# Holding the first input transfers behind the first weight split, and moving two groups of small products, in a one-core decoder layer

## The chip, the core and the metric

The kernel runs on one core of a Trainium2 chip. The core has a matrix engine (TensorE, PE in the profile; its loads of stationary operands are PEld), a vector engine (VectorE, DVE), a scalar engine (ScalarE, ACT), a general engine (GpSimd, POOL) and an engine that here issues nearly all transfers (SyncE, SP). Each engine runs its own list of instructions in a fixed order and waits on semaphores for the others. The metric is device time in microseconds, the median of the runs shown. A change of 0.2% (2.4 us here) is about what can be told from no change.

## The reference

One layer of a decoder trunk on 1024 tokens of width 1024, float32:

```python
h = rmsnorm(x, norm1_w)
proj = h @ w_in                      # q, k, v, z, beta, gate of mixer A; q, k, v of mixer B
qkv_a = silu(causal_dwconv(qkv_a, conv_qkv_w))      # 4 taps
qa, ka = l2norm(qa) * 128**-0.5, l2norm(ka)
o_a = gated_delta_rule(qa, ka, va, g, beta)         # 4 heads of 128, chunks of 64
o_a = rmsnorm(o_a, gdn_norm_w) * silu(z)
o_b = dilated_attention(qb, kb, vb)                 # 8 heads of 64, 3 windows
x = x + concat(o_a, o_b) @ w_out
u = causal_dwconv(rmsnorm(x, norm2_w) @ w_up, ffn_conv_w)   # 3 taps
x = x + (silu(gate) * up) @ w_down
return rmsnorm(x, final_norm_w)
```

The change touches the first norm, the projection to the first three keys of mixer A, and the start of the delta rule.

## The kernel before, in words

Every large product of float32 operands is made as three products of rounded parts: each operand is split into a high part (`...hi`, a copy on ACT) and a low part (`...lo`, the difference on DVE), and PE adds high x high, high x low and low x high. Channels lie on partitions, tokens along the free axis. So a 128x128 weight block against 512 tokens costs three products of 128x512.

The stretch up to about 70 us runs as follows.

- **Loads.** The input comes as eight channel tiles `xt` (128 channels x 1024 tokens, 512 KB; the first in two halves), the weights of the first three keys as four pairs `wst` (two channel blocks x 384 columns, 384 KB; the first pair in two halves of 192 KB). Each engine that issues transfers feeds its own queue. The two halves of the first weights leave from ACT, everything else from SP.
- **Splits.** `split_first` splits weights, `split_x` splits an input tile and scales it with `norm1_w` on the way. Squares of the tiles (`sq`) are summed into `acc` on DVE for the norm.
- **First products.** Before its data is there PE runs nine products `warm`. `first()` then adds, channel tile by channel tile, six accumulators (three keys x two halves of the tokens): 18 products for each tile.
- **Norm and gates.** `norms()` sums `acc` over the channels with eight small products (`ps<-ones,acc`), POOL raises the result to -0.5 (`rst`), PE spreads it over the partitions by eight transposes (`ps<-ident,rst`), and DVE copies that out as `rstdB`. `gates()` makes decay and beta from `wba` and the unscaled tiles (`ps<-xt,wba`), then `ps<-sel,barow` and `ps<-g,tri`.
- **Keys.** DVE multiplies each accumulator by `rstdB` (`xr`). `conv_silu` then makes a key: ACT scales by the first tap (`kT<-xr,gcw`), DVE adds three taps (`kT<-xr,gcw,kT`), ACT takes a tanh (`xr<-kT`), DVE finishes (`kT<-xr,kT`). `kprep(h)` takes the finished key: `tokens()` transposes it on PE (`ps<-ident,kT`, two halves of four), ACT copies each half out and squares it (`ktok`, `sq`), DVE makes the scales (`ssk`, `bp`, `ke`), and PE multiplies the key with itself in two halves of four (`ps<-kT`), which DVE turns into `um`. On the side POOL masks the decay rows `dec` and ACT takes their exponentials. All transposes and key products of this stage share two PSUM banks of the tag `atr`.
- **Dense products.** Between these small pieces PE works through the products of the remaining weights, which begin with the fourth key and then the values.

What sets the order: `Weave` is a planner that runs while the kernel is recorded. It keeps a clock of PE and estimated ready times of tiles (`need`) and of banks (`slot_free`); each stream of work is a generator that yields the time it still has to wait, with `slack` added. The order in which streams reach PE in that plan is the order of PE's instructions (each gets an issue order token). On ACT, DVE, POOL and SP the order is set by the scheduler of the framework, with `ua` and `uv` for work of high priority and `after(a, b)` for pairs that must keep an order. `A(name, tag)` takes a slot of a tag; a slot is reused in turn, and a transfer into it waits for the last reader of its former content. The four weight pairs take turns in the two slots of the tag `wst`.

Of the kernel before, what the change touches and what calls it, by code (L numbers as in the profile page):

```python
# [7 lines left out]
F32 = mybir.dt.float32  # L8
# [7 lines left out]
P = 128  # L16
# [4 lines left out]
FT = 22  # L21
NEG = -1.0e30
APART = 0.5
KSLACK = 1.0
EPS = 1e-6
SLOTS = {"kT": 2, "kU": 2, "dv": 2, "dw": 2, "kt": 4, "uy": 5, "qa": 4, "ev": 2, "go": 2, "Xa": 7, "Xb": 9}
TURNS = {"kT*": ("kT", "kU"), "dv*": ("dv", "dw"), "X": ("Xa",) * 7 + ("Xb",) * 9}
# [120 lines left out]
def hybrid_layer(tc, I, out):  # L148
    nc = tc.nc
    wv = Weave()  # L150
# [5 lines left out]
    po_ = Engine(wv, nc.gpsimd, "gpsimd", 0.15, 0.0021)  # L156
    sy = Engine(wv, nc.sync, "sync", 0.05, 0.00142, 2.2)
    sa = Engine(wv, nc.scalar, "actq", 0.05, 0.00142, 2.2)
    es = ExitStack()
    cp = es.enter_context(tc.tile_pool(name="cp", bufs=1))  # L160
    wp = es.enter_context(tc.tile_pool(name="wp", bufs=1))
# [5 lines left out]
    def tile_(pool, shape, dt, name, tag, bufs):  # L167
        return wv.slot(pool.tile(list(shape), dt, name=name, tag=tag, bufs=bufs), tag, bufs)
# [3 lines left out]
    def A(name, tag, dt=F32, shape=(P, 1024)):  # L172
        if tag in TURNS:
            i = turns[tag] = turns.get(tag, -1) + 1
            tag = TURNS[tag][i % len(TURNS[tag])]
        return tile_(lp, shape, dt, name, tag, SLOTS[tag])

    def X(name, dt=F32R):
        return A(name, "X", dt)
# [7 lines left out]
    order = mybir.DependencyInfo(mybir.DependencyClass.NoSync, mybir.DependencyReason.DATA)  # L187

    def after(inst, anchor, reason="keeps a slot free until it is needed"):
        tc.add_manual_dep(inst.ins, anchor.ins.name, order, reason=reason)  # L190
# [83 lines left out]
    def half(i):  # L274
        return slice(i * 512, i * 512 + 512)
# [8 lines left out]
    acc = A("acc", "go")  # L284
    wk0 = []

    def split_x(xt, k, sl):
        hi, lo = xs[k]
        inst = ua.activation(hi[:, sl], xt[:, sl], AF.Copy, scale=n1[:, k:k + 1])
        if k == 0:  # L290
            after(inst, his[0] if sl.start else whis[0], "in the order of arrival")
        if k == 1:
            after(inst, whis[1], "the weights come first")
        his[k:] = [inst]
        lo_of[0] = uv.scalar_tensor_tensor(lo[:, sl], xt[:, sl], n1[:, k:k + 1], hi[:, sl].bitcast(F32), op0=OP.mult,
                                           op1=OP.subtract)

    def split_first(src, hi, lo):
        whis.append(ua.activation(hi, src, AF.Copy))
        return uv.tensor_tensor(lo, src, hi.bitcast(F32), op=OP.subtract)  # L300

    his, los, lo_of, sqs, whis = [], [], [None], [], []
# [11 lines left out]
    for k in range(KT):  # L314
        xt = A("xt", ("kT*", "dv*")[k % 2])
        xts.append(xt)
        if k % 2 == 0:
            wst = tile_(wp, [P, 2, 384], F32, "wst", "wst", 2)
            whi, wlo = [A(nm, "uy", F32R, (P, 2, 384)) if k < 4 else A(nm, "kt", F32R, (P, 2, 384))
                        for nm in ("whi", "wlo")]  # L320
            wk0.append((whi, wlo))
        xs.append((X("xhi"), X("xlo")))
        if k == 0:
            for j in range(2):
                sa.dma_start(wst[:, j, :], I["w0"][0, :, j])
            for h in range(2):
                sy.dma_start(xt[:, half(h)], I["xT"][:P, half(h)])
            split_first(wst[:, 0, :], whi[:, 0, :], wlo[:, 0, :])
            for h in range(2):
                split_x(xt, 0, half(h))  # L330
            split_first(wst[:, 1, :], whi[:, 1, :], wlo[:, 1, :])
        else:
            if k % 2 == 0:
                sy.dma_start(wst, I["w0"][k // 2])
            sy.dma_start(xt, I["xT"][k * P:(k + 1) * P, :])
            if k % 2 == 0:
                split_first(wst, whi, wlo)
            split_x(xt, k, slice(0, S))
        los.append(lo_of[0])
        if k > 1:  # L340
            square(k - 2, his[k], los[k])
# [55 lines left out]
    rstdB = const("rstdB", [P, S])  # L397

    def norms():
        yield wv.need(acc, slack=9.5)  # L400
        ssp = yield from next_bank("atr", acc)
        for c in range(NCH):
            mm(ssp[:, c:c + 1], acc[:, c * P:(c + 1) * P], ones[:, :1], 0.215)
            if c % 2:
                yield APART
        ve.tensor_scalar(rst, ssp[:, :NCH], 1.0 / 1024, EPS, op0=OP.mult, op1=OP.add)
        rsqrt(rst, rst, NCH)
        wv.done.add("rst")
        yield wv.need(rst)
        for h in range(2):  # L410
            if h:
                yield wv.need(rstdB, slack=0.3)
            pb = yield from next_bank("atr")
            for c in range(4):
                i = 4 * h + c
                tp(pb[:, c * P:(c + 1) * P], rst[:, i:i + 1].to_broadcast([P, P]))
            ve.tensor_copy(rstdB[:, half(h)], pb)
        wv.done.add("norms")
# [211 lines left out]
    def kprep(h):  # L630
# [44 lines left out]
        for c0 in range(0, NCH, 4):  # L675
            pt = yield from next_bank("atr", slack=KSLACK * (c0 == h == 0))
            for c in range(4):
# [1007 lines left out]
```

## Time and profile before

| | |
|---|---|
| median of 3 runs | 1202.02 us (1200.88 to 1202.2) |
| profiled execution, its own time | 1201.61 us |
| span of that execution, first to last instruction | 1199.6 us |
| granted clock of PE over the span | 0.998 |
| PE busy | 1186.8 us, 99% |
| DVE, ACT, POOL busy | 915.6, 574.8, 87.2 us |
| DMA moved | 154.80 MB, 129 GB/s on average |
| DMA from 8 to 12 us | 417 GB/s |

All times of the trace count from the start of the span. In a row of the timeline stand start, length, engine, line, operation, output and inputs, shapes, count, and in brackets the idle time of the engine just before it with what ended that idle time. The operations recorded through the `Engine` helper all carry line 142 or 144, and those of PE line 193 or 197, so they are told apart by their tiles. Products overlap: a product of 128x512 shows 0.39 us, while the next starts 0.227 us after it.

### The profile page before, as it was taken

The page shows a single profiled execution, that of the slowest core. Times are in us where ns is not written, and L with a number is a line of the kernel's source. Part 1 is how long each engine was busy: PE and PEld are TensorE (multiplying, and loading weights), DVE is VectorE, ACT ScalarE, POOL GpSimd, SP SyncE. Part 2 cuts the span into 40 slices and gives each one's busy share as a digit, 9 for nine tenths or more (in the row PEclk, how much of TensorE's full clock was granted, in tenths as well). Part 3 has the DMA queues.
Part 4 walks back from the last instruction along what each step waited for, and adds up shares of the span by engine and source line. Part 5 has one row for each costly group of instructions (what it writes and reads, how often), then busy time and mean ns, then how long its engine had stood idle before and what let it go on. Part 6 is the DMA issues. An engine that isn't in the chain of part 4 may idle for free.

```text
span 1199.6 us, 18291 instructions
## 1 busy us (share of the span) xinstructions
PE 1186.8 (99%) x7050; PEld 983.1 (82%) x7050; DVE 915.6 (76%) x1450; ACT 574.8 (48%) x1126; POOL 87.2 (7%) x90
## 2 busy tenths in 40 slices
PE   9999999999999999999999999999999999999997
PEld 7788888888777778888888888888888888888886
DVE  7683975666365566777989988989888889999875
ACT  7375344355454443655544544445454454434441
POOL 0212010214311120000000000000000000000000
PEclk9999999999999999999999999999999999999999
DMA  7424334435634204443213223131222398557514
GB/s 234 110 87 122 109 118 129 141 123 171 224 100 124 80 28 129 163 158 122 88 53 105 83 76 105 54 105 56 103 87 72 101 375 295 187 159 225 166 54 140
DMA packets 85799, 154.80 MB, mean 129 GB/s; under 512 B 21169, under 2 KB 36305, under 8 KB 85713
## 3 DMA queue, kind: packets, MB, share of 16 engines
q1 hardware_dynamic: 84704, 152.72, 39.4%
q8 instruction: 55, 0.90, 0.3%
q10 hardware_dynamic: 1008, 0.92, 0.2%
q14 instruction: 32, 0.25, 0.1%
HBM read 117.68 MB, written 35.93 MB: 128 GB/s over the span
## 4 chain that ended last, share of the span: by engine, by line
PE 93%; DVE 2%; DMA 1%; ACT 1%; issue 1%; SPq 0%; POOLq 0%; POOL 0%; DVEq 0%; ACTq 0%
PE ps L193 44%; PE pa L193 20%; PE dw L193 17%; PE pc L193 10%; PE ps L197 3%; DVE kT L142 1%; DMA xt<-in_xT 1%; ACT sm L144 0%; DVE xr L142 0%; DMA alog<-in_a_log 0%; DMA n<-in_n 0%; DVE x1h L142 0%; PE pd L193 0%; DVE zz L142 0%; ACT dec L142 0%
## 5 line engine op out<-in xcount | busy, mean ns | idle before, releaser
L193 PE MATMUL dw<-pr 128*128 128x512 f32 (+1 forms) x984 | 211.3, 376 | 0.0
L193 PEld LDWEIGHTS dw<-pr 128*128 128x128 f32 x984 | 176.7, 188 | 33.6
L193 PE MATMUL ps<-xhi,whi 128*128 128x512 f32 x384 | 157.3, 410 | 0.9 <-ACT xhi L144 0.9
L193 PE MATMUL ps<-xhi,wlo 128*128 128x512 f32 x384 | 150.2, 391 | 0.8 <-DVE wlo L144 0.8
L193 PE MATMUL ps<-xlo,whi 128*128 128x512 f32 x384 | 148.4, 390 | 0.0
L193 PE MATMUL pa<-T,pair 128*128 128x512 f32 x528 | 127.1, 389 | 0.0
L193 PEld LDWEIGHTS pa<-T,pair 128*128 128x128 f32 x528 | 99.0, 188 | 20.6
L193 PEld LDWEIGHTS ps<-xhi,whi 128*128 128x128 f32 x384 | 72.2, 188 | 19.9 <-issue 5.6
L193 PEld LDWEIGHTS ps<-xhi,wlo 128*128 128x128 f32 x384 | 72.1, 188 | 16.8 <-DVE wlo L144 1.2
L193 PEld LDWEIGHTS ps<-xlo,whi 128*128 128x128 f32 x384 | 72.4, 188 | 12.4
L142 ACT ACTIVATE u<-pa 128x512 f32<-128x512 f32 x44 | 26.3, 598 | 107.3 <-PE pa L193 107.3
L142 DVE SCALAR_TENSOR_TENSOR y<-xu,fcw,y 128x1023 f32<-128x1023 f32 (+1 forms) x44 | 56.4, 1281 | 22.1 <-ACT y L142 22.0
L142 ACT ACTIVATE whi<-wst 128x1024 fp32r<-128x1024 f32 x36 | 38.3, 1063 | 67.8 <-PE ps L193 55.0
L193 PE MATMUL pa<-B,A 128*128 128x512 f32 x264 | 63.4, 389 | 0.0
L193 PE MATMUL pc<-T,S 128*128 128x512 f32 x264 | 63.4, 389 | 0.0
L193 PE MATMUL pa<-T,S 128*128 128x512 f32 x264 | 63.4, 389 | 0.0
L193 PE MATMUL pc<-B,pair 128*128 128x512 f32 x264 | 63.4, 389 | 0.0
L142 DVE TENSOR_TENSOR wst<-wst 128x512 f32<-128x512 f32 x88 | 60.6, 688 | 0.9
L193 PE MATMUL ps<-B,pair 128*128 128x512 f32 x252 | 60.5, 389 | 0.0
L144 ACT ACTIVATE sm<-sm,mx 128x128 f32<-128x128 f32 (+7 forms) x64 | 35.4, 555 | 47.9 <-DVE mx L144 47.9
L142 ACT ACTIVATE pr<-wd 128x1024 fp32r<-128x1024 f32 x33 | 34.9, 1057 | 48.8 <-PE dw L193 38.9
L142 POOL TENSOR_TENSOR rs<-rs,mhalf 128x2 f32<-128x2 f32 (+2 forms) x4 | 4.5, 1116 | 738.7 <-DVE rs L144 738.7
(246 smaller groups left out, 2408.3 us busy)
## 6 DMA issues: line engine op xcount, KB each, us to landing
wst<-in_wu SPq DMA_DIRECT2D x44, 512.0 KB, 3.7
wd<-in_wd SPq DMA_DIRECT2D x44, 512.0 KB, 4.5
upark<-y SPq DMA_DIRECT2D x22, 512.0 KB, 3.7
wst<-in_wi SPq DMA_DIRECT2D x21, 512.0 KB, 3.7
r<-upark SPq DMA_DIRECT2D x11, 512.0 KB, 7.4
r<-upark SPq DMA_DIRECT2D x22, 256.0 KB, 7.5
wa<-in_wd SPq DMA_DIRECT2D x22, 256.0 KB, 3.5
wst<-in_wv SPq DMA_DIRECT2D x8, 512.0 KB, 3.7
```

What stands on the lines that cost most here:

```text
L142: return getattr(eng, op)(*a, **kw)
L144: return getattr(eng, op)(*a, **kw)
L193: tc.stamp_issue_order_token(nc.tensor.matmul(dst, lhs, rhs, start=start, stop=stop, **kw).ins, TOKEN)
L197: tc.stamp_issue_order_token(nc.tensor.transpose(dst, src, ident if idt is None else idt).ins, TOKEN)
```

## The change

Five things change.

1. `KSLACK`, the slack with which the planner places the first half of the first key's product with itself after a bank comes free, goes from 1.0 to 2.2.
2. The slack with which the planner places the norm's sums `ps<-ones,acc` goes from 9.5 to 11.0.
3. The first weight half leaves first, from SP. The first input tile's halves leave from SP and ACT, and the second weight half follows from SP.
4. The third and fourth weight pairs get slots of the tag `ev` instead of taking turns in `wst`.
5. Ahead of each later transfer of an input tile or of a weight pair, POOL copies one column of the first split weights (`whi` of the first pair) into the tile that is to be loaded. The transfer overwrites it, and so has to wait for that copy, and the copy for the first split on ACT. One more `after` asks that the third weight pair's high part on ACT comes after the second tile's.

```diff
@@ -21,7 +21,7 @@
 FT = 22
 NEG = -1.0e30
 APART = 0.5
-KSLACK = 1.0
+KSLACK = 2.2
 EPS = 1e-6
 SLOTS = {"kT": 2, "kU": 2, "dv": 2, "dw": 2, "kt": 4, "uy": 5, "qa": 4, "ev": 2, "go": 2, "Xa": 7, "Xb": 9}
 TURNS = {"kT*": ("kT", "kU"), "dv*": ("dv", "dw"), "X": ("Xa",) * 7 + ("Xb",) * 9}
@@ -297,6 +297,8 @@
 
     def split_first(src, hi, lo):
         whis.append(ua.activation(hi, src, AF.Copy))
+        if len(whis) == 3:
+            after(whis[2], his[1], "in the order of arrival")
         return uv.tensor_tensor(lo, src, hi.bitcast(F32), op=OP.subtract)
 
     his, los, lo_of, sqs, whis = [], [], [None], [], []
@@ -315,23 +317,27 @@
         xt = A("xt", ("kT*", "dv*")[k % 2])
         xts.append(xt)
         if k % 2 == 0:
-            wst = tile_(wp, [P, 2, 384], F32, "wst", "wst", 2)
+            wst = tile_(wp, [P, 2, 384], F32, "wst", "wst", 2) if k < 4 else A("wst", "ev", shape=(P, 2, 384))
             whi, wlo = [A(nm, "uy", F32R, (P, 2, 384)) if k < 4 else A(nm, "kt", F32R, (P, 2, 384))
                         for nm in ("whi", "wlo")]
             wk0.append((whi, wlo))
         xs.append((X("xhi"), X("xlo")))
         if k == 0:
-            for j in range(2):
-                sa.dma_start(wst[:, j, :], I["w0"][0, :, j])
-            for h in range(2):
-                sy.dma_start(xt[:, half(h)], I["xT"][:P, half(h)])
+            sy.dma_start(wst[:, 0, :], I["w0"][0, :, 0])
+            for h, queue in enumerate((sy, sa)):
+                queue.dma_start(xt[:, half(h)], I["xT"][:P, half(h)])
+            sy.dma_start(wst[:, 1, :], I["w0"][0, :, 1])
             split_first(wst[:, 0, :], whi[:, 0, :], wlo[:, 0, :])
             for h in range(2):
                 split_x(xt, 0, half(h))
             split_first(wst[:, 1, :], whi[:, 1, :], wlo[:, 1, :])
         else:
+            if k and k % 2 == 0:
+                po_.tensor_copy(wst[:, 0, :1], wk0[0][0][:, 0, :1].bitcast(F32))
             if k % 2 == 0:
                 sy.dma_start(wst, I["w0"][k // 2])
+            if k:
+                po_.tensor_copy(xt[:, :1], wk0[0][0][:, 0, :1].bitcast(F32))
             sy.dma_start(xt, I["xT"][k * P:(k + 1) * P, :])
             if k % 2 == 0:
                 split_first(wst, whi, wlo)
@@ -397,7 +403,7 @@
     rstdB = const("rstdB", [P, S])
 
     def norms():
-        yield wv.need(acc, slack=9.5)
+        yield wv.need(acc, slack=11.0)
         ssp = yield from next_bank("atr", acc)
         for c in range(NCH):
             mm(ssp[:, c:c + 1], acc[:, c * P:(c + 1) * P], ones[:, :1], 0.215)
```

Since the order is made by a planner and a scheduler, the diff alone does not tell where instructions stand. Two places follow.

**The loads.** SP's list from its first transfer on, before. `xt` with 128x512 is a half of the first input tile, `wst` with 128x768 a weight pair:

```order
L142 DMA xt_92<-in_xT 128x512 x2
L142 DMA xt_110<-in_xT 128x1024
L142 DMA wst_117<-in_w0 128x768
L142 DMA xt_116<-in_xT 128x1024
L142 DMA xt_130<-in_xT 128x1024
L142 DMA xt_139<-in_xT 128x1024
L142 DMA xt_154<-in_xT 128x1024
L142 DMA xt_163<-in_xT 128x1024
L142 DMA xt_178<-in_xT 128x1024
L142 DMA ident_193<-in_ident 128x128
```

The same place now, where `wst` with 128x384 is a half of the first weight pair:

```order
L142 DMA wst_93<-in_w0 128x384
L142 DMA xt_92<-in_xT 128x512
L142 DMA wst_93<-in_w0 128x384
L142 DMA ident_203<-in_ident 128x128
L142 DMA xt_110<-in_xT 128x1024
L142 DMA wst_118<-in_w0 128x768
L142 DMA xt_117<-in_xT 128x1024
L142 DMA xt_133<-in_xT 128x1024
L142 DMA wst_144<-in_w0 128x768
L142 DMA xt_143<-in_xT 128x1024
```

The two first weight halves are now on SP, the identity matrix `ident` has come ahead of the later tiles, the first pair that follows stands behind the second input tile, and from the fifth row on each transfer waits for a copy on POOL.

DVE's list around the split of the third weight pair, whose low part is `wlo_142` before:

```order
L142 TENSOR_SCALAR gw2_209<-gnw_203 128x1
L144 TENSOR_SCALAR xlo_168<-xt_163,n1_72,xhi_167 128x1024
L142 TENSOR_TENSOR acc_91<-acc_91,sq_175 128x1024
L142 TENSOR_TENSOR wba_211<-wba_211,n1_72 128x8x8
L144 TENSOR_TENSOR wlo_142<-wst_140,whi_141 128x768
L144 TENSOR_SCALAR xlo_180<-xt_178,n1_72,xhi_179 128x1024
L142 TENSOR_TENSOR acc_91<-acc_91,sq_184 128x1024
```

Now, where the same part is `wlo_146` (and `xlo_148` belongs to the fifth input tile):

```order
L144 TENSOR_SCALAR xlo_135<-xt_133,n1_72,xhi_134 128x1024
L142 TENSOR_TENSOR acc_91<-sq_131,sq_140 128x1024
L144 TENSOR_TENSOR wlo_146<-wst_144,whi_145 128x768
L144 TENSOR_SCALAR xlo_148<-xt_143,n1_72,xhi_147 128x1024
L142 TENSOR_TENSOR acc_91<-acc_91,sq_157 128x1024
L144 TENSOR_SCALAR xlo_162<-xt_160,n1_72,xhi_161 128x1024
```

The third pair's split has moved from behind the seventh input tile (`xlo_168`) to ahead of the fifth.

**The keys.** PE's list after the transposes of the first finished key, from the last of the eighteen dense products that follow them, before. `kT_490` is the first key; `whi_474` and `whi_601` are weights of the dense products:

```order
L193 MATMUL ps_600<-whi_474,xhi_111 128x512
L193 MATMUL ps_600<-wlo_475,xhi_111 128x512
L193 MATMUL ps_600<-whi_474,xlo_112 128x512
L193 MATMUL ps_709<-kT_490 128x128 x4
L193 MATMUL ps_597<-whi_601,xhi_120 128x512
L193 MATMUL ps_597<-wlo_602,xhi_120 128x512
L193 MATMUL ps_597<-whi_601,xlo_121 128x512
L193 MATMUL ps_598<-whi_601,xhi_120 128x512
L193 MATMUL ps_598<-wlo_602,xhi_120 128x512
L193 MATMUL ps_598<-whi_601,xlo_121 128x512
L193 MATMUL ps_726<-kT_490 128x128 x4
```

Now, where `kT_564` is the second key (`kT_554` in the list before), and the first key is `kT_500`:

```order
L193 MATMUL ps_610<-whi_484,xhi_111 128x512
L193 MATMUL ps_610<-wlo_485,xhi_111 128x512
L193 MATMUL ps_610<-whi_484,xlo_112 128x512
L197 MATMUL ps_721<-ident_203,kT_564 128x128 x4
L193 MATMUL ps_607<-whi_611,xhi_121 128x512
L193 MATMUL ps_607<-wlo_612,xhi_121 128x512
L193 MATMUL ps_607<-whi_611,xlo_122 128x512
L197 MATMUL ps_738<-ident_203,kT_564 128x128 x4
L193 MATMUL ps_608<-whi_611,xhi_121 128x512
L193 MATMUL ps_608<-wlo_612,xhi_121 128x512
L193 MATMUL ps_608<-whi_611,xlo_122 128x512
```

Where the first key's product stood, PE now has the transposes of the second key. The first key's product has moved behind those of the other keys.

ACT's list at the same place, before. `xr_484<-kT_554` is the tanh of the second key, `ktok` and `sq` read the transposed first key, and `kT_590` is the fourth key:

```order
L142 ACTIVATE xr_484<-kT_554 128x1024
L144 ACTIVATE ktok_627<-ps_628 128x512
L144 ACTIVATE sq_634,ssk_626<-ps_628 128x128
L144 ACTIVATE sq_636,ssk_626<-ps_628 128x128
L144 ACTIVATE sq_638,ssk_626<-ps_628 128x128
L144 ACTIVATE sq_640,ssk_626<-ps_628 128x128
L144 ACTIVATE ktok_627<-ps_642 128x512
L144 ACTIVATE sq_648,ssk_626<-ps_642 128x128
L144 ACTIVATE sq_650,ssk_626<-ps_642 128x128
L144 ACTIVATE sq_652,ssk_626<-ps_642 128x128
L144 ACTIVATE sq_654,ssk_626<-ps_642 128x128
L142 ACTIVATE kT_590<-xr_542,gcw_201 128x1024
```

Now, where `kT_600` is the fourth key and `xr_494<-kT_564` the tanh of the second:

```order
L142 ACTIVATE kT_600<-xr_552,gcw_211 128x1024
L144 ACTIVATE ktok_637<-ps_638 128x512
L144 ACTIVATE sq_644,ssk_636<-ps_638 128x128
L144 ACTIVATE sq_646,ssk_636<-ps_638 128x128
L144 ACTIVATE sq_648,ssk_636<-ps_638 128x128
L144 ACTIVATE sq_650,ssk_636<-ps_638 128x128
L144 ACTIVATE ktok_637<-ps_652 128x512
L144 ACTIVATE sq_658,ssk_636<-ps_652 128x128
L144 ACTIVATE sq_660,ssk_636<-ps_652 128x128
L144 ACTIVATE sq_662,ssk_636<-ps_652 128x128
L144 ACTIVATE sq_664,ssk_636<-ps_652 128x128
L142 ACTIVATE xr_494<-kT_564 128x1024
```

The tanh of the second key and the scaling of the fourth key have changed places: the tanh now stands behind the reading of the first key's transposes.

## The prediction

> **What bounds the kernel now.** I read the page's busy times first, then the list of waits on PE, then the timeline of PE at those waits, and last ACT and DVE around the first keys.
>
> ```profile
> PE 1186.8 (99%) x7050; PEld 983.1 (82%) x7050; DVE 915.6 (76%) x1450; ACT 574.8 (48%) x1126; POOL 87.2 (7%) x90
> ...
> PE ps L193 <- ACT xhi L144: 0.9, 1, 0.9
> PE ps L193 <- DVE wlo L144: 0.8, 1, 0.8
> PE ps L193 <- ACT sq L144: 0.6, 1, 0.6
> PE ps L193 <- ACT w L144: 0.5, 1, 0.5
> PE ps L193 <- DVE ct L144: 0.5, 1, 0.5
> ```
>
> PE is busy for 1186.8 of 1199.6 us and no product is removed. So the change can take away only PE's idle time, about 3 us of which lies where it acts, and any new wait on PE is paid in full. These are the places in PE's timeline:
>
> ```profile
> 1.10 4.21 PE L193 MATMUL warm<-warm 128*128 128x128 f32 x18 [1.10 <-DVE ones L142]
> 6.20 0.50 PE L193 MATMUL ps<-xhi,whi 128*128 128x512 f32 x1 [0.88 <-ACT xhi L144]
> 6.54 0.40 PE L193 MATMUL ps<-xhi,wlo 128*128 128x512 f32 x1
> ...
> 22.88 0.39 PE L193 MATMUL ps<-xlo,whi 128*128 128x512 f32 x1
> 24.09 0.50 PE L193 MATMUL ps<-xhi,wlo 128*128 128x512 f32 x1 [0.83 <-DVE wlo L144]
> ...
> 41.80 0.60 PE L197 MATMUL ps<-ident,rst 128*128 128x128 f32 x4
> ...
> 61.77 1.03 PE L197 MATMUL ps<-ident,kT 128*128 128x128 f32 x8
> ...
> 66.52 0.39 PE L193 MATMUL ps<-whi,xlo 128*128 128x512 f32 x1
> 67.52 1.16 PE L193 MATMUL ps<-kT 128*128 128x128 f32 x8 [0.61 <-ACT sq L144]
> ```
>
> From 6.54 to 22.88 stand 72 products at 16.34 / 72 = 0.227 us each, without a gap. The waits are 0.88 us before the first product, 0.83 us for the third weight pair, and 0.61 us at the first key's product, whose PSUM bank ACT still reads.
>
> **Part 1, the first loads: -0.85 us.**
>
> ```profile
> xt<-in_xT SPq DMA_DIRECT2D x1, 256.0 KB, 2.8
> ...
> wst<-in_w ACTq DMA_DIRECT2D x1, 192.0 KB, 3.8
> ...
> wst<-in_wi SPq DMA_DIRECT2D x1, 512.0 KB, 3.4
> ...
> 5.01 0.52 ACT L144 ACTIVATE whi<-wst 128x384 fp32r<-128x384 f32 x1 [1.59 <-DMA wst<-in_w]
> 5.44 1.32 ACT L144 ACTIVATE xhi<-xt,n 128x512 fp32r<-128x512 f32 x2
> ```
>
> ACT waits for the first weight half, 3.8 us under way from ACT's queue. The first transfer on SP took 2.8 us from 0.72, so the half lands near 3.5 and is split by 4.0. The tile's first half is now second on SP: if it needs as long as that first weight half did, it lands by 1.15 + 3.8 = 4.95 and is split by 5.65. With 2.8 us it is split by 4.7, before `warm` ends at 5.31. I take 5.35 for the first product instead of 6.20; the bounds are 0.5 and 0.89 us gained.
>
> The second tile now waits for the first split, a POOL copy of one column and SP's issue: about 4.0 + 0.3 + 0.1 = 4.4. Alone on the queue, 512 KB took 3.4 us, so it lands near 7.8 and its high part is ready near 9.0. PE wants it after 18 products, at 5.35 + 18 x 0.227 = 9.4. This costs nothing, but the cover is 0.4 us, and it is a rival below. Behind the waiting transfers SP holds all small constants; the one PE meets first is `wba`, for the gates.
>
> ```profile
> wba<-in_wba SPq DMA_DIRECT2D x1, 32.0 KB, 4.4
> ...
> 27.26 1.92 PE L193 MATMUL ps<-xt,wba 128*32 128x512 f32 x16
> ```
>
> Its eight products stand six products earlier than before, so at 27.26 - 1.7 - 1.4 = 24.2 with the gains of parts 1 and 2. The transfer leaves once the seventh tile has landed, near 17, and lands near 21.5. That is free with 2.7 us to spare.
>
> **Part 2, slots for the third and fourth weight pairs: -0.83 us.** They are split ahead of the fifth and the seventh tile instead of behind later work, and the transfer waits for no slot, so the wait at 24.09 goes. The bound is all of it or, if DVE is held up by something else, none. The nine POOL copies and PE's order otherwise cost PE nothing: POOL is idle until 38 us. Together, PE is 1.7 us ahead from here on.
>
> **Part 3, the norm's sums and the first keys: a new wait.** The sums move back among the products, and the transposes of `rst` three groups (nine products, 2.0 us): 41.80 + 2.0 - 1.7 = 42.1. DVE's copy of `rstdB` therefore comes at about the old time, near 43.2. These rows give what follows on DVE:
>
> ```profile
> 43.47 0.68 DVE L142 COPY rstdB<-ps 128x512 f32<-128x512 f32 x1
> 44.94 0.69 DVE L142 COPY rstdB<-ps 128x512 f32<-128x512 f32 x1 [0.79 <-PE ps L197]
> ...
> 46.31 0.69 DVE L142 TENSOR_TENSOR xr<-ps,rstdB 128x512 f32<-128x512 f32 x1 [0.19 <-PE ps L193]
> 47.26 0.18 DVE L142 TENSOR_SCALAR ngam<-ngam 128x32 f32<-128x32 f32 x1 [0.26 <-ACT ngam L142]
> 49.74 1.28 DVE L142 SCALAR_TENSOR_TENSOR kT<-xr,gcw,kT 128x1023 f32<-128x1023 f32 x1
> 50.94 0.69 DVE L142 TENSOR_TENSOR xr<-ps,rstdB 128x512 f32<-128x512 f32 x1
> ...
> 52.73 2.11 DVE L142 SCALAR_TENSOR_TENSOR kT<-xr,gcw,kT 128x1022 f32<-128x1022 f32 x1
> ...
> 60.08 1.22 DVE L142 SCALAR_TENSOR_TENSOR kT<-xr,kT 128x1024 f32<-128x1024 f32 x1 [0.59 <-ACT xr L142]
> ```
>
> Before, 6.27 us pass from the first copy to the first tap at 49.74, of which 0.79 + 0.19 + 0.26 = 1.24 are waits. Now the sixth `xr` (0.6 us) is ahead of the taps too, and I leave 0.1 of the waits: 43.2 + 5.03 + 0.6 + 0.1 = 48.9. From the first tap to the finished first key it took 61.30 - 49.74 = 11.56 us; without that `xr` 10.96. Three of its taps took 2.11 instead of 1.28 us while POOL masked `dec`; one such overlap fewer would save 0.83. So the first key is finished at E = 59.0 to 59.9; I take 59.5. PE reaches its transposes at 61.77 - 1.7 = 60.1 and does not wait for it.
>
> Then comes what decides. PE does the eight transposes and eighteen dense products, done at 66.52 + 0.23 - 1.7 = 65.05, and next stand the transposes of the second key. That key's tanh on ACT now stands behind the reading of the first key's transposes:
>
> ```profile
> 61.42 2.45 ACT L142 ACTIVATE dec<-dec,ngc 128x128 f32<-128x128 f32 x8 [1.37 <-DVE gel L142]
> ...
> 64.93 1.05 ACT L142 ACTIVATE xr<-kT 128x1024 f32<-128x1024 f32 x1
> 65.88 0.58 ACT L144 ACTIVATE ktok<-ps 128x512 f32<-128x512 f32 x1
> ...
> 68.83 1.19 ACT L142 ACTIVATE kT<-xr,gcw 128x1024 f32<-128x1024 f32 x1
> 69.87 0.24 ACT L142 ACTIVATE ge<-gel 128x8 f32<-128x8 f32 x1
> ```
>
> Before, ACT starts `dec` at E + 0.12 (E was 61.30) and ends the squares 7.41 us later, at 68.83, with the tanh inside (0.95 us, 64.93 to 65.88). Now the fourth key's scaling is inside instead (1.04 us, 68.83 to 69.87): 7.50. Then follow the tanh, 1.05, and DVE's last step, 1.22. The second key is finished at E + 0.12 + 7.50 + 1.05 + 1.22 = E + 9.9 = 69.4 (68.9 to 69.8). PE waits there for 69.4 - 65.05 = 4.3 us. Before, PE went on at 67.52 from the same point, with all the same work done. So at the keys the kernel is 69.4 - 67.52 = 1.9 us behind, gains included. The same by its parts: -0.85 - 0.83 - 0.61 + 4.3 = +2.0, less 0.16 that lay between 66.75 and 67.52 beside the wait of 0.61.
>
> **Later.** The order also shifts in the chain of states around 250 to 280 us, where the two waits of 0.5 us for `ct` and `w` stand. They could both go (-1.0) or double (+1.0). PE comes 1.9 us later to products whose inputs hang on its own order, so I expect one more such wait: +0.5. Past that the order is the same.
>
> Sum: +1.9 + 0.5 = +2.4 us on 1201.61 us, the profiled execution's own time (span 1199.6 and 2.0 around it): 1204.0. The median of the runs, 1202.02, lies 0.4 above that execution, so I forecast 1204.4.
>
> **Rivals.**
>
> *The clock falls in the new gap.* The only long lull of PE is at the end:
>
> ```profile
> 1187.82 2.44 PE L193 MATMUL dw<-pr 128*128 128x256 f32 x19
> ...
> 1192.00:1194.00 2.00, 0.43 (x2) 0.19 (x2) 0.70 (x3) 0.00 (x0) 0.69 (x1) 0.92 0.38 128
> 1194.00:1196.00 2.00, 0.00 (x0) 0.00 (x0) 2.00 (x6) 0.00 (x0) 0.00 (x0) 0.50 0.57 191
> ```
>
> In the last two rows (two windows of 2 us) stand the busy times of PE, PEld, DVE, ACT and POOL, then the granted clock. The last dense products end at 1190.26. A mean of 0.92 over 1192 to 1194 and 0.50 after it puts the fall to half at 1193.68, some 3.4 us later, although a few small products came between. The new wait is 4.3 us, so a fall is possible. Its price is a stretch at half clock. `warm` shows such a stretch: 4.21 / 18 = 0.234 us for a pass, against at most 1.16 / 8 = 0.145 for the same shape at the keys. If it lasts as long again, half of 4.21 is lost: +2.1, so 1206.5. For it speaks that 4.3 is more than 3.4. Against it, that this one lull is all the evidence, and that the new wait exceeds it by 0.9 us only. The Trainium skill, "TensorE: Matmul & The Clock Gate", section "What's actually happening", says that an idle window of about 3.4 us halves the clock, and that the windows run freely. By that page a gap of 4.3 us holds a whole window with an estimated chance of (4.3 - 3.4) / 3.4, about one in four. The end of this trace agrees with the 3.4 us.
>
> *The second key is ready in time.* Then only the gains remain: -0.85 - 0.83 - 0.61 = -2.3 us, so 1199.7, faster. It decides for faster or no change once the second key is finished before 65.05 + 2.3 = 67.3, that is 2.1 us earlier than I have it. For it: ACT is only half busy, and were its 2.45 us of exponentials of `dec` behind the tanh, that alone would do. Against it: ACT's list has them ahead, and with E at 59.0 only 0.5 of the 2.1 us is found.
>
> *The second tile comes late.*
>
> ```profile
> xt<-in_xT SPq DMA_DIRECT2D x7, 512.0 KB, 8.5
> ```
>
> In the old, full queue the tiles were 8.5 us under way. If the second one takes not 3.4 but 5.3 us, it lands at 9.7 and PE waits for it. Everything over the 0.4 us of cover delays PE, the norm and both keys alike: +1.5, so 1205.9. For it: three transfers issued before it may still be under way at 4.4. Against it: they carry under 0.6 MB between them, and it has no other queue beside it.
>
> *The held transfers do nothing*, because the first loads land when they did: the first product stays at 6.20. Since E follows PE, the end is 0.85 later than forecast, 1205.2; this lies in the range.
>
> **How the numbers follow.** Chances: the new wait at full clock 0.46, with the clock falling 0.28, second tile late or no gain at the start 0.14, second key in time 0.12. The likeliest gives 1204.4, with its own range 1202.9 to 1205.9 (E by 0.45 either way, the later waits by 0.5 to 1.0). For 8 in 10 the range reaches into the case of the clock above and to the edge of the gain below: 1202.2 to 1207.3. The bound of 0.2% lies at 1204.4, in the middle of the first case: it gives 0.26 slower and 0.20 the same. The clock gives 0.27 slower, the late tile 0.13 slower. The key in time gives 0.09 faster. Small parts and shifts of the runs go to the middle. Slower 0.66, same 0.24, faster 0.10.
>
> **What would show it.** Right: the first product near 5.35 with no wait for `xhi`, no wait for `wlo` near 22, the second tile's `xhi` on ACT before 9.4, and a wait of about 4 us on PE before `ps<-ident,kT`, released by DVE's `kT`, near 69. The granted clock in the windows behind it tells the first rival. Wrong: no such wait, a wait for `xhi` near 9.4, or a wait at `ps<-xt,wba`.

## The result and the profile after

The changed kernel takes **1206.93 us** (median of six runs, 1206.24 to 1207.91), the kernel before 1201.93 us beside it. The ratio is 1.0042 (95% interval 1.003 to 1.0055): slower by 5.0 us. The profiled execution took 1207.54 us, with a span of 1205.7 us and a granted clock of 0.994.

The busy times of the page and the list of PE's waits, after:

```profile
PE 1190.7 (99%) x7050; PEld 985.8 (82%) x7050; DVE 914.2 (76%) x1450; ACT 573.9 (48%) x1126; POOL 88.0 (7%) x100
```

```profile
PE ps L197 <- DVE kT L142: 3.9, 1, 3.9
...
PE ps L193 <- ACT w L144: 0.9, 2, 0.5
PE ps L193 <- ACT xhi L144: 0.3, 1, 0.3
```

The waits for `wlo` and for the first key's `sq` are gone, and one wait of 3.9 us for a key has come. PE has the same 7050 products, but is busy 3.9 us longer. So part of the loss is no wait at all: some products became slower. PE's timeline shows where:

```profile
5.60 0.79 PE L193 MATMUL ps<-xhi,whi 128*128 128x512 f32 x1 [0.29 <-ACT xhi L144]
6.19 0.63 PE L193 MATMUL ps<-xhi,wlo 128*128 128x512 f32 x1
6.62 0.43 PE L193 MATMUL ps<-xhi,whi 128*128 128x512 f32 x1
6.89 0.39 PE L193 MATMUL ps<-xhi,wlo 128*128 128x512 f32 x1
...
60.59 1.03 PE L197 MATMUL ps<-ident,kT 128*128 128x128 f32 x8
...
65.33 0.39 PE L193 MATMUL ps<-whi,xlo 128*128 128x512 f32 x1
69.62 1.11 PE L197 MATMUL ps<-ident,kT 128*128 128x128 f32 x4 [3.90 <-DVE kT L142]
...
73.94 0.63 PE L193 MATMUL ps<-whi,xhi 128*128 128x512 f32 x1
74.37 0.63 PE L193 MATMUL ps<-wlo,xhi 128*128 128x512 f32 x1
74.80 0.47 PE L193 MATMUL ps<-whi,xlo 128*128 128x512 f32 x1
75.11 0.39 PE L193 MATMUL ps<-whi,xhi 128*128 128x512 f32 x1
75.33 0.39 PE L193 MATMUL ps<-wlo,xhi 128*128 128x512 f32 x1
```

Behind the wait, products of 128x512 start 0.43 us apart, and from 75.11 on again 0.22 to 0.23 us. The windows of 2 us (busy times of PE, PEld, DVE, ACT, POOL, then the granted clock, DMA's share and GB/s) say why:

```profile
66.00:68.00 2.00, 0.00 (x0) 0.00 (x0) 0.54 (x3) 2.00 (x10) 0.35 (x1) 1.00 0.61 229
68.00:70.00 2.00, 0.38 (x2) 0.38 (x3) 1.84 (x5) 1.57 (x4) 1.29 (x1) 0.53 0.04 16
70.00:72.00 2.00, 2.00 (x8) 1.60 (x7) 2.00 (x4) 2.00 (x8) 0.00 (x0) 0.50 0.03 8
72.00:74.00 2.00, 2.00 (x9) 1.71 (x8) 1.24 (x2) 2.00 (x11) 0.00 (x0) 0.50 0.49 92
74.00:76.00 2.00, 2.00 (x8) 1.63 (x7) 0.56 (x4) 2.00 (x11) 0.48 (x1) 0.76 0.42 170
```

The clock is halved. A mean of 0.53 puts the fall at 68.00 + 2 x 0.06 = 68.12, the 0.76 puts the rise at 74.96: 6.84 us at half clock, of which PE worked 69.62 to 74.96.

A table of where PE stands is the best summary. It gives how much later than in the kernel before PE starts the same product in the profiled execution of each kernel: the first key's transposes (`ps<-ident,kT`, 61.77 before), the first transposes of a query (`ps<-ident,qT`, 138.98), the first product of the output projection (`ps<-ohi`, 468.04), and the whole span (1199.6). "Loads" means the three edits to the transfers and slots.

| kernel | first key | first query | projection | span | median, us |
|---|---|---|---|---|---|
| the change: loads, norm 11.0, KSLACK 2.2 | -1.18 | +4.63 | +5.41 | +6.1 | 1206.93 |
| e1: loads, norm 11.0 | -1.05 | -1.47 | -1.47 | -1.2 | 1200.22 |
| e2: KSLACK 2.2 alone | +0.26 | +1.87 | +2.89 | +3.2 | 1204.84 |
| e5: loads, KSLACK 2.2 | -0.05 | +1.43 | +2.29 | +2.5 | 1204.31 |
| e6: loads alone | +7.17 | +7.02 | +7.00 | +7.3 | 1201.92 |
| e3: the change, gap filled | -0.96 | +3.28 | +4.13 | +4.6 | 1205.16 |
| e4: the change, tanh earlier | -1.42 | +3.28 | +4.09 | +4.3 | 1205.71 |
| e10: the change, gap filled in part | -1.02 | +3.99 | +4.89 | +5.4 | 1206.77 |
| e7: e1 without slots | -0.69 | -0.88 | -0.85 | -0.6 | 1200.12 |
| e8: e1 without holds | -1.71 | -1.79 | -1.52 | -1.5 | 1200.95 |
| e9: e1 without slots and holds | -1.45 | -1.52 | -1.48 | -1.4 | 1200.32 |

One of the six executions of e10, 1700.12 us at a mean clock of 0.653, is left out of its median. The row of e6 is one of the executions in which the clock fell ahead of the first key (below). Differences of some tenths in the column "first key" say little: even among the seven kernels with the same loads (the change and e1, e3, e4, e5, e6, e10) the first product row with `xlo` starts anywhere from 7.14 to 7.82 us, and the lead of e8 and e9 stands already there (7.01 and 7.26). The change gains 1.2 us up to the first key, loses 5.8 us from there to the first query, and another 1.5 us later. The median of the kernel before was 1202.45 us beside e1 to e4, 1201.99 beside e5 to e8 and 1202.14 beside e9 and e10.

### The profile page after: what moved, and what is told of

It reads as the page before. It is cut to its first block, busy times and chain, and to the rows that moved or that the text cites. A ratio compares the mean times of both kernels' runs of the same rounds, so it can differ in the third digit from the quotient of the medians.

```text
span 1205.7 us, 18326 instructions
## 1 busy us (share of the span) xinstructions
PE 1190.7 (99%) x7050; PEld 985.8 (82%) x7050; DVE 914.2 (76%) x1450; ACT 573.9 (48%) x1126; POOL 88.0 (7%) x100
## 4 chain that ended last, share of the span: by engine, by line
PE 95%; DVE 2%; ACT 2%; issue 1%; DMA 0%; POOLq 0%; POOL 0%; DVEq 0%; SPq 0%; ACTq 0%
PE ps L193 45%; PE pa L193 20%; PE dw L193 17%; PE pc L193 10%; PE ps L197 3%; DVE kT L142 1%; ACT sm L144 0%; ACT whi L142 0%; DMA xt<-in_xT 0%; DVE x1h L142 0%; PE pd L193 0%; DVE zz L142 0%; ACT dec L142 0%; ACT xr L142 0%; ACT sq L144 0%
## 5 line engine op out<-in xcount | busy, mean ns | idle before, releaser
L142 ACT ACTIVATE whi<-wst 128x1024 fp32r<-128x1024 f32 x36 | 38.2, 1063 | 69.4 <-PE ps L193 58.3
L193 PEld LDWEIGHTS pa<-B,A 128*128 128x128 f32 x264 | 49.6, 188 | 10.3
```

The source lines that it names most:

```text
L142: return getattr(eng, op)(*a, **kw)
L193: tc.stamp_issue_order_token(nc.tensor.matmul(dst, lhs, rhs, start=start, stop=stop, **kw).ins, TOKEN)
```

## The experiments

**Which edit makes the new order at the keys?** Two runs take one number each, one out of the change and one alone.

e1, against the changed kernel:

```diff
-KSLACK = 2.2
+KSLACK = 1.0
```

> The changed kernel with KSLACK back at 1.0; loads, slots and the norm's slack stay as changed. In PE's list the first key's product stands ahead of the second key's transposes again. Theory (the new order at the keys carries the loss: 3.3 us of restart and 2.5 us of half clock, while the loads gain 1.2 us at the first key's transposes): no wait of PE on kT, granted clock 1.00 from 66 to 80 us, and 1201.9 - 1.2 - 0.5 (the wait for sq, shorter since the first key is finished 2.6 us earlier and PE only 1.2) = 1200.2, between 1199.7 and 1201.2. Rival (the held loads or the later sums of the norm carry it): 1205 or more.

Measured: 1200.22 us (1199.57 to 1202.4), a ratio of 0.9989 to the kernel before (0.998 to 0.9998). No wait on `kT`, and the clock is 1.00 throughout this stretch. PE's timeline:

```profile
60.72 1.03 PE L197 MATMUL ps<-ident,kT 128*128 128x128 f32 x8
...
66.05 1.16 PE L193 MATMUL ps<-kT 128*128 128x128 f32 x8 [0.20 <-ACT sq L144]
```

The wait at the first key's product is 0.20 us where it was 0.61 before. So with the rest of the change in place one number carries the whole loss, and the rest is a small gain: 2.2 us on the kernel before, with an interval that just excludes no change. ACT's order, however, stays that of the changed kernel:

```profile
64.41 0.58 ACT L144 ACTIVATE ktok<-ps 128x512 f32<-128x512 f32 x1
...
67.36 1.08 ACT L142 ACTIVATE xr<-kT 128x1024 f32<-128x1024 f32 x1
```

The second key is finished as late as 70.5 us here too, but PE comes to its transposes only at 75.48, and nothing waits.

e2, against the kernel before:

```diff
-KSLACK = 1.0
+KSLACK = 2.2
```

> The kernel before with KSLACK at 2.2 and nothing else. Theory: PE ends its eighteen products at 66.75 us, the second key is finished 9.9 us behind the first, 61.3 + 9.9 = 71.2, a wait of 4.4 us; less the 0.8 us that stood at the first key's product before, plus 2.5 us of half clock and 0.8 us later: 1201.9 + 6.9 = 1208.8, between 1207.8 and 1209.8; without the fall of the clock 1206.3. Rival (loads or norm carry the loss): 1202.

Measured: 1204.84 us (1204.05 to 1205.74), ratio 1.0023 (1.0013 to 1.0033). Slower, but by another way than expected. There is no wait on `kT`, and the clock stays up. PE's waits and two rows of ACT's timeline:

```profile
PE ps L197 <- ACT sq L144: 0.8, 2, 0.6
PE ps L193 <- ACT sq L144: 0.5, 2, 0.3
```

```profile
65.19 1.05 ACT L142 ACTIVATE xr<-kT 128x1024 f32<-128x1024 f32 x1
66.14 0.57 ACT L144 ACTIVATE ktok<-ps 128x512 f32<-128x512 f32 x1
```

Here the second key's tanh (`xr<-kT`) still stands ahead of `ktok`. The order on PE is the new one, but the second key is in time, and PE waits for the two banks instead, at four places (0.62, 0.16, 0.27, 0.27 us in the timeline; one place with 0.61 before). PE loses 1.6 us up to the first query and 1.0 us later. The four waits account for 0.7 us of the 1.6 (1.32 against 0.61 before); which pauses make the rest is not shown. My expectation had taken over ACT's order from the changed kernel.

**What puts the tanh behind?** In the changed kernel ACT's timeline has it the other way round:

```profile
64.27 0.58 ACT L144 ACTIVATE ktok<-ps 128x512 f32<-128x512 f32 x1
...
67.22 1.09 ACT L142 ACTIVATE xr<-kT 128x1024 f32<-128x1024 f32 x1
```

e5, against the changed kernel:

```diff
-        yield wv.need(acc, slack=11.0)
+        yield wv.need(acc, slack=9.5)
```

> The changed kernel with the norm's slack back at 9.5; KSLACK stays at 2.2. PE's list at the keys stays as changed, but on ACT the second key's tanh stands ahead of the reading of the first key's transposes again. Theory (the wait of 3.9 us needs both numbers, KSLACK for PE's order and the norm's slack for ACT's): no wait of PE on kT and granted clock 1.00 from 66 to 80 us. What stays is the new order of PE, as with KSLACK alone: 1.87 - 0.26 = 1.6 us from the first key's transposes to the first q and 1.0 us later, less the 1.2 us of the loads: 1202.45 + 1.4 = 1203.9. The sums of the norm move 9 products ahead, to about 33.37 - 2.6 - 0.7 = 30.1 us, while DVE ended acc at 31.6: up to 1.5 us of wait for acc more. So 1203.4 to 1205.4. Rival (KSLACK alone makes the wait, the run with KSLACK alone escaped it by its later loads): a wait on kT of 2 us or more and a half clock, 1206 or more.

Measured: 1204.31 us, ratio 1.0031 (1.0016 to 1.0046), no wait on `kT`, clock 1.00 from 66 to 80 us. The tanh stands ahead of `ktok` again (64.80 against 65.75 us). So with the loads as changed the wait of 3.9 us takes both numbers: KSLACK moves the second key's transposes forward on PE (e1), the norm's slack moves the second key's tanh back on ACT. That order on ACT is there in every run with 11.0 and in none with 9.5, except that e4 forces another. Each alone leaves the second key in time for PE. No run has both numbers without the loads. The wait for `acc` that the expectation named is there too:

```profile
PE ps L193 <- DVE acc L142: 1.2, 1, 1.2
```

e6 takes both numbers back, so that the loads are alone:

```diff
-KSLACK = 2.2
+KSLACK = 1.0
@@
-        yield wv.need(acc, slack=11.0)
+        yield wv.need(acc, slack=9.5)
```

> The changed kernel with both numbers back (KSLACK 1.0, norm 9.5): the loads and slots alone. Theory (both numbers act on the order only; the loads gain 1.2 us at the first key's transposes): no wait on kT, none of wlo. If PE reaches the norm's sums near 30.1 us, as worked out from 33.37 - 2.6 - 0.7, and acc is done at 31.6 as now, a wait of 1.5 us at ps<-ones,acc eats the gain: 1202.4; if acc comes earlier too, 1200.2 or, with the wait for sq gone, 1199.8. Between 1199.6 and 1202.6; I take 1201.3. Rival (the loads bring nothing by themselves, the norm's slack did it): 1202.4 without a wait at ones,acc.

Measured: a median of 1201.92 us, ratio 1.0015 (0.9999 to 1.003), no verdict. But the twelve executions lie in two groups: eight between 1200.97 and 1202.04, four between 1207.76 and 1208.72 with a granted clock of 0.991 to 0.992. The profiled execution is one of the four. Its timeline and windows:

```profile
33.43 0.58 PE L193 MATMUL ps<-ones,acc 128*128 128x1 f32 x4 [1.85 <-DVE acc L142]
```

```profile
32.00:34.00 2.00, 0.57 (x5) 0.60 (x6) 1.28 (x2) 0.00 (x0) 0.00 (x0) 1.00 0.63 168
34.00:36.00 2.00, 2.00 (x11) 1.67 (x11) 0.00 (x0) 0.00 (x0) 0.00 (x0) 0.81 0.51 201
36.00:38.00 2.00, 2.00 (x11) 1.91 (x10) 0.00 (x0) 0.00 (x0) 0.00 (x0) 0.50 0.00 0
...
48.00:50.00 2.00, 2.00 (x10) 1.80 (x9) 0.94 (x3) 0.00 (x0) 0.00 (x0) 0.78 0.04 8
```

With the loads earlier, PE reaches the norm's sums before DVE has summed `acc`, and waits 1.85 us. That alone eats most of the gain: the eight have a median of 1201.55 us, against 1201.99 before. In the profiled execution the clock fell on top of it, from 35.24 to 48.88 us, 13.64 us long; half of it, 6.8 us, is close to the 6.6 us between the medians of the two groups, so the other three with that granted clock most likely did the same. In e5, whose wait is 1.2 us, three of twelve executions (1210.89 to 1211.12 us) show such a clock too, 0.991 to 0.992. So with the loads the norm's slack of 11.0 is what makes their gain usable: it keeps PE from arriving at `acc` too early (e1 has no such wait). It hurts only together with KSLACK at 2.2. The norm's slack alone, without the loads, was not run.

**How much is the clock?** e3 puts work into the gap. Its output is that of the changed kernel, since the transposes overwrite the bank.

```diff
             pt = yield from next_bank("atr", src)
+            if hh == 0 and src is T.get(("k", 1)):
+                for _ in range(14):
+                    mm(pt[:, :P], ident, ident, 0.0)
             for c in range(4):
```

> The changed kernel with 14 more products ident x ident (128x128) on PE just ahead of the second key's transposes, into the bank that these overwrite; the output is untouched. The bank is free when the first four squares are done, near 66.0 us, and 14 products at 1.16 / 4 = 0.29 us at most, 0.23 us in a row, last 3.2 to 4.1 us, so PE is busy from 66.0 to 69.2 or 70.1. Theory (a lull of PE halves the clock, the wait itself stays): the transposes start at 69.6 to 70.1, the granted clock stays 1.00, and 2.5 us of half clock go: 1204.4, between 1204.0 and 1205.2. Rival (the loss behind 70 us has another cause than the lull): 1206.9 or, with fillers too long, 1207.4.

Measured: 1205.16 us (1204.57 to 1206.15), ratio to the kernel before 1.0029 (1.0018 to 1.0041). PE's timeline:

```profile
67.01 3.39 PE L193 MATMUL ps<-ident 128*128 128x128 f32 x28 [1.07 <-ACT sq L144]
70.73 0.66 PE L197 MATMUL ps<-ident,kT 128*128 128x128 f32 x4 [0.33 <-DVE kT L142]
```

The clock stays at 1.00. From the first key to the first query PE loses 3.28 + 0.96 = 4.24 us instead of 4.63 + 1.18 = 5.81. The second key's transposes stand 9.92 us behind the first key's (70.73 - 60.81) instead of 9.03 (69.62 - 60.59), so a wait that is 0.89 us longer is hidden in it. The clock's share is 5.81 - 4.24 + 0.89 = 2.5 us. That agrees with the timeline: 5.34 us of work at half clock could have cost 2.67 at most. The rival, another cause behind 70 us, falls.

**Can the wait be taken away on ACT?** e4 asks ACT for the second key's tanh ahead of `ktok`:

```diff
             if dst is not None and scale is None:
-                ua.activation(dst[:, half(hh)], pt, AF.Copy)
+                inst = ua.activation(dst[:, half(hh)], pt, AF.Copy)
+                if hh == 0 and src is T["k", 0]:
+                    after(inst, kends[1][0])
```

> The changed kernel with the second key's tanh on ACT ahead of the reading of the first key's transposes; PE's list stays word for word that of the changed kernel. The tanh starts at 64.3 instead of 67.2 us, DVE ends the second key near 67.2 at the latest (its tap for the third key may come first), so PE waits 0.8 to 1.6 us instead of 3.9. Theory (the wait stands for ACT's order, and only a long lull halves the clock): the clock stays 1.00, 2.3 to 3.1 us of wait and 2.5 us of half clock go, 1206.9 - 5.2 = 1201.7, between 1201.2 and 1202.2. Rival (any wait of this place halves the clock): 1204.2. Rival (PE's order itself costs, later on): 1203 or more at full clock.

Measured: 1205.71 us (1203.87 to 1207.62), ratio 1.0033 (1.0021 to 1.0046). The edit missed its aim: in the trace the tanh ran at 66.27 us, between the two halves of the reading, not at 64.3. So the wait shrank to 3.15 us only, and the clock fell all the same:

```profile
66.00:68.00 2.00, 0.00 (x0) 0.00 (x0) 0.85 (x2) 2.00 (x9) 0.00 (x0) 1.00 0.86 229
68.00:70.00 2.00, 1.36 (x7) 1.17 (x8) 2.00 (x6) 2.00 (x10) 0.00 (x0) 0.81 0.13 41
70.00:72.00 2.00, 2.00 (x9) 1.60 (x7) 2.00 (x3) 2.00 (x8) 1.90 (x1) 0.50 0.00 0
72.00:74.00 2.00, 2.00 (x9) 1.65 (x8) 0.79 (x4) 2.00 (x11) 0.64 (x1) 0.83 0.64 233
```

It fell at 69.24, when PE had been back at work for 0.6 us (the transposes start at 68.64), and rose at 72.68: 3.44 us. With 1205.71 us the run also missed the 1201.2 to 1202.2 that was expected. It doesn't settle what a short wait would cost, but it shows that a lull shorter than 3.4 us is enough.

e10 asks that more closely, with 5 products of filling in place of 14:

```diff
-                for _ in range(14):
+                for _ in range(5):
```

> The changed kernel with 5 instead of 14 more products ident x ident ahead of the second key's transposes. From 65.6 us on PE idles 1.1 to 1.4 us (bank), works 3.39 x 5 / 14 = 1.2 us, and idles again 1.2 to 1.5 us until DVE's kT, ready 69.6 to 70.4. Theory A (the clock falls after a window of 3.4 us in which PE idled about half or more, as in the loads-alone run, where 1.85 us of wait sufficed in 4 of 12 runs): windows with up to 2.6 us of idling occur here too, so some runs lose 1.7 or 3.4 us to the half clock and others nothing: 1204.5 to 1208, granted clocks of the runs from 0.994 to 0.998. Theory B (only an unbroken lull longer than about 3 us halves it): 1204.3 in all runs, all at 0.997 to 0.998.

Measured: five executions between 1205.92 and 1207.99 us, median 1206.77, ratio to the kernel before 1.0042 (1.0029 to 1.0055). Timeline and windows:

```profile
66.07 1.38 PE L193 MATMUL ps<-ident 128*128 128x128 f32 x10 [0.19 <-ACT sq L144]
69.79 0.66 PE L197 MATMUL ps<-ident,kT 128*128 128x128 f32 x4 [2.33 <-DVE kT L142]
```

```profile
70.00:72.00 2.00, 2.00 (x11) 1.66 (x10) 2.00 (x2) 2.00 (x8) 0.00 (x0) 0.63 0.04 8
72.00:74.00 2.00, 2.00 (x7) 1.61 (x6) 1.42 (x3) 2.00 (x12) 0.00 (x0) 0.52 0.45 96
```

An unbroken wait of 2.33 us halved the clock, from 70.52 to 73.92: 3.40 us. Theory B falls. The spread of 2.1 us over the five fits theory A, but none of them reached the 1204.5 that it allowed for an execution without a fall.

**What gains on the way to the first key?** e7, e8 and e9 take parts of the loads out of e1.

e7:

```diff
-            wst = tile_(wp, [P, 2, 384], F32, "wst", "wst", 2) if k < 4 else A("wst", "ev", shape=(P, 2, 384))
+            wst = tile_(wp, [P, 2, 384], F32, "wst", "wst", 2)
```

> The run with KSLACK back, and the third and fourth weight pairs in the two slots of wst again; the held loads stay. PE's list is the same word for word. Theory (the slots removed the wait for wlo): a wait of 0.8 us or more comes back, at the third or at the fourth pair, and its pause of 0.2 us: PE is 1.0 us later at the first key's transposes, 1200.2 + 0.6 to 1.0 = 1201.0, between 1200.6 and 1202.2. Rival (the held order of the loads removed it): no such wait, 1200.2.

e8:

```diff
-            if k and k % 2 == 0:
-                po_.tensor_copy(wst[:, 0, :1], wk0[0][0][:, 0, :1].bitcast(F32))
...
-            if k:
-                po_.tensor_copy(xt[:, :1], wk0[0][0][:, 0, :1].bitcast(F32))
```

> The run with KSLACK back, without POOL's copies that hold the later transfers; the order of the first four transfers and the slots stay. Theory (the copies bring the first product from about 6.2 to 5.6 us, but most of that lies at half clock): the first product at 5.9 to 6.3 us, the third product within 0.4 us of where it was, and the end within 0.4 us, 1200.2 to 1200.6. The planner shifts the sums of the norm by some rows. Rival (the copies carry the gain of the loads): 1201.2 or more. Rival (the copies cost time on the way): 1199.8 or less.

e9 makes both edits at once:

> The run without holds, and also without slots: of the change to the loads only the order of the first four transfers and the one after are left (KSLACK 1.0, norm 11.0). Each of slots and holds was dispensable alone. Theory A (the first loads in their new order are split earlier, and that alone frees DVE for the third weights in time): no wait for wlo or one below 0.3 us, 1200.2 to 1201.2. Theory B (one of slots or holds is needed): the wait for wlo is back with 0.6 us or more, and the time is 1201.2 to 1202.4.

Measured: 1200.12, 1200.95 and 1200.32 us, with ratios to the kernel before of 0.9988 (0.9979 to 0.9996), 0.9993 (0.9984 to 1.0002) and 0.9987 (0.9979 to 0.9996). None has a wait for `wlo` in PE's list. DVE's timeline has the third pair's low part at these places, in the kernel before, in e7 and in e9:

```profile
23.08 0.95 DVE L144 TENSOR_TENSOR wlo<-wst,whi 128x768 fp32r<-128x768 f32 x1
```

```profile
22.37 0.95 DVE L144 TENSOR_TENSOR wlo<-wst,whi 128x768 fp32r<-128x768 f32 x1
```

```profile
19.52 0.95 DVE L144 TENSOR_TENSOR wlo<-wst,whi 128x768 fp32r<-128x768 f32 x1
```

What the three have in common, the order of the first four loads, the one added `after` and the norm's slack of 11.0, is enough to get DVE there in time. Neither the slots nor POOL's copies are needed. e6 lost the wait at a slack of 9.5, with slots and copies, so the slack is not the likely cause, but order, `after` and slack were not taken apart. (The `after` acts on the third high part that `split_first` makes; the first pair makes two, so that is the second weight pair's, not the third's as the list of the change has it.) With the holds but without the slots (e7) the low part is only just in time, and PE stands 0.36 us behind e1 at the first key, 0.2 of which it had lost before. Theory A of e9 holds, and in e7 the rival held. e8 met neither side: its first product came at 5.52 us, earlier than the 5.9 to 6.3 of the theory, and its time lies between the 1200.6 of the theory and the 1201.2 of the rival.

## Why the prediction was right and wrong

The forecast was 1204.4 us in a range of 1202.2 to 1207.3, slower with a chance of 0.66. Measured is 1206.93: slower, in the range, but by the case that I held for the second likeliest. The likeliest case alone ended at 1205.9; the result is in the range because the range was drawn on into that rival. Going by the steps, on the profiled execution:

| step | forecast, us | measured, us |
|---|---|---|
| first loads | -0.85 | -0.10 |
| third weights | -0.83 | -1.08 |
| PE reaches the second key | 65.05 | 65.56 |
| first key finished | 59.5 | 58.72 |
| second key's transposes | 69.4 | 69.62 |
| the new wait, from 65.05 and 65.56 | 4.3 | 4.1, of which 3.9 idle |
| restart, against 67.52 before | +1.9 | +2.1 |
| half clock | 0, or +2.1 in the rival | +2.5 |
| later | +0.5 | +1.5 |
| span | +2.4 | +6.1 |

- **The new wait: right in place, cause and releaser, its size partly by luck.** The chain from ACT's `dec` to the finished second key took 9.83 us (59.73 to 69.56) against 9.77 in the prediction. But two errors ahead of it cancel. The first key was finished 0.78 us earlier than forecast, and `dec` started 1.01 us behind it instead of 0.12, since it waited for DVE's small copy `gel`, which took 1.06 us instead of 0.16. Before and after:

```profile
61.23 0.16 DVE L142 COPY gel<-dec 128x8 f32<-128x8 f32 x1
```

```profile
58.63 1.06 DVE L142 COPY gel<-dec 128x8 f32<-128x8 f32 x1
59.73 2.46 ACT L142 ACTIVATE dec<-dec,ngc 128x128 f32<-128x128 f32 x8 [2.27 <-DVE gel L142]
```

The slow copy fell into a stretch in which POOL masked `dec` (57.65 to 60.71 us), the fast one did not; that POOL is the cause was not tested. What the prediction also didn't see is that this wait needs two of the edits together (e1 and e5); it treated them as one part.

- **The clock: the step that failed.** "Against it, that this one lull is all the evidence, and that the new wait exceeds it by 0.9 us only" took 3.4 us for the length of the lull that is needed. It isn't. Waits of 3.90, 3.15 and 2.33 us all halved the clock, and one of 1.85 us did so too, in a kernel where the clock fell in four of twelve executions. With 2.3 us as the length, the fall would have been the likeliest case for a wait of 4.3 us, and the rival's own sum, 1206.5, the forecast. Its price of 2.1 came close to the measured 2.5 by luck: it is half of the 4.21 us of `warm`, whereas the half clock lasted 6.84 us here, with 5.34 us of work in it.
- **The first loads: the term was mis-sized.** The first product came at 5.60, not 5.35, and from there it gained nearly nothing: the next starts 0.59, 0.43 and 0.27 us apart instead of 0.34 and 0.23. A spacing of 0.43 is that of the half-clock stretch at 74 us, so the clock had not risen yet, although the profile's clock column reads 1.00 in these first windows. The first row with `xlo` starts only 0.10 us earlier (7.59 against 7.69). How much is gained hangs on when the clock rises. In e8 it rises while `warm` still runs, whose eighteen passes take 3.69 us there and 4.21 in the changed kernel, the next product follows 0.34 us behind the first, and 0.68 us are kept up to the first row with `xlo`:

```profile
1.10 3.69 PE L193 MATMUL warm<-warm 128*128 128x128 f32 x18 [1.10 <-DVE ones L142]
5.52 0.50 PE L193 MATMUL ps<-xhi,whi 128*128 128x512 f32 x1 [0.72 <-ACT xhi L144]
5.86 0.40 PE L193 MATMUL ps<-xhi,wlo 128*128 128x512 f32 x1
```

- **The second tile: right.** Its high part was started at 7.90 us, and PE never waited for it. That rival had no part in the result.
- **The third weights: the right size with the wrong cause.** The wait and the pause around it (0.98 us together) went, but not because of the slots (e7, e9).
- **Later: too small.** From the first query to the projection PE loses 0.78 us, to the end of the span 0.69 more. With KSLACK back (e1) nothing is lost up to the projection, with KSLACK alone (e2) 1.02 us, so KSLACK's order makes that part; the part behind it varies from 0.2 to 0.7 us over the runs. The prediction expected one more wait like those for `w` and `ct`. These don't grow (0.9 us against 1.0), so which pauses cost the time stays open.

The sum closes: -0.10 - 1.08 + 3.28 (from -1.18 to +2.10 at the restart) + 2.53 (to +4.63) + 0.78 + 0.69 = 6.1 us.

## What to carry to other kernels

When PE is nearly always busy, price a new wait with the clock in mind: here each of the three waits of 2.3 us or more ahead of dense work brought a stretch at half clock that cost about another 1.7 to 2.5 us (half of its length, or of the work in it), and even one of 1.85 us led to a fall. Test edits that steer a planner one by one and in pairs, because a number for one engine's order can be harmless until another number has moved a second engine. And a gain that brings PE earlier to its next input is worth only what that input's own chain allows: here the loads' gain needed the norm's sums moved back to be kept.

## What the runs showed of the hardware

The half-clock stretches were 3.40, 3.44, 6.84 and 13.64 us long, that is 1, 1, 2 and 4 times 3.41. The fall came 0.6 to 1.8 us after PE had resumed in e4, e6 and e10, and 1.5 us before it in the changed kernel. That fits a clock set anew every 3.4 us by what PE did in the stretch just past: the last such stretch before each fall holds 2.4 us of idling in the changed kernel (65.72 to 68.12), 2.8 in e4 by the same count, 2.3 in e10 and 1.6 in e6.

The ends of these traces bear this out. The granted clock falls a last time when the kernel runs out of products: at 1197.96 us in the changed kernel, 1199.08 in e4, 1200.32 in e10 and 1199.16 in e6, read from the windows as above. Counted from the rise before it (74.96, 72.68, 73.92 and 48.88) that is 1123.0, 1126.4, 1126.4 and 1150.3 us. These distances differ by 0, 3.4, 23.9 and 27.3 us, which is 0, 1, 7 and 8 times 3.41, though PE's work behind the rises has no such steps. The start of the changed kernel fits too: 18 times 3.41 us before the fall at 68.12 lies 6.7, where the spacing of the first products turns from 0.43 to 0.27. So in these four executions the clock seems to change only at marks 3.41 us apart, which the waits do not shift. That would explain why a first product 0.6 us earlier gained only 0.1 us.

The Trainium skill, "TensorE: Matmul & The Clock Gate", section "What's actually happening", says that free-running windows of about 3.4 us decide. These four lengths and the marks agree. Its section "HAM oscillation — how this bites in real kernels" gives as the rule to avoid idle gaps over some 3.4 us. The falls after 2.33 and 1.85 us differ from that: a window need not be idle as a whole.

In e6 the clock came back late. It stayed low for four such stretches although PE shows as busy in all of them; between 35 and 46 us its list mixes dense products with the small ones of the norm and the gates. In the kernel before the same mixture left the clock at 1.00. What it takes for the clock to come back stays open. The times of the changed kernel's six runs, 1206.24 to 1207.91, spread over 1.67 us, about half of 3.4 us: what one stretch more or less at half clock costs. That this is the cause of the spread was not shown for each run.
